# Expert pairs of a hybrid block: the combination moved behind the gathers, other accumulator banks first, and gate and up in four runs

## The chip, the cores and the metric

One core of a Trainium2 chip runs the whole program. The metric is device time in microseconds (us) of one execution; the time before is the median of three runs. PE is TensorE (PEld its weight loads), DVE is VectorE, ACT is ScalarE, POOL is GpSimd, SP is SyncE, which issues the weight loads.

## What is computed

A transformer block on 512 tokens of width 1024 in float32: an mLSTM branch and a forgetting-attention branch that are merged, a cross attention, and a mixture of 32 experts of which each token uses two, with a last normalisation. The change lies in the experts:

```python
for e in range(N_EXPERTS):                                  # 32
    he = jax.nn.silu(t @ w_gate[e]) * (t @ w_up[e])         # 1024 -> 512
    y = y + combine[:, e:e + 1] * (he @ w_down[e])          # 512 -> 1024
```

`t` is the normalised input, and `combine` holds each token's weight for each expert, zero for all but two.

## The kernel before

The parts ahead of the experts (branches, attention, router) end at about 790 us of the span and are not touched. The experts run as 16 pairs (`NPAIR`), loop at L1108. An expert takes at most 64 tokens (`CAP`) in a pass, so the two experts of a pair lie side by side in the 128 columns or partitions of one tile. A further loop for experts with more tokens follows the pairs and is not entered in the profiled execution.

For each pair PE does five kinds of work:

- **Gather** (`stationary`, L1012): the tokens of the next pair are picked out of the normalised input `xn` by a matmul with a matrix of zeros and ones, `G` (made by POOL, L1030). A call handles four of the eight blocks of 128 input channels with 32 matmuls (L1019) into one `pss` bank; DVE then scales it to `st` (L1021). Two calls a pair.
- **Gate and up** (`gate_up`, L1037): 16 steps. A step multiplies one block of channels of both experts' tokens with a row block of each expert's matrix; the two matmuls of a step use 64 columns of the array each and run side by side (L1044, `64x512` in the order, `128*64` in the profile, where each matmul has two records). Steps 0 to 7 take gate for the first expert and up for the second, steps 8 to 15 the other two. The results stay in two `acc` banks until all 16 are done.
- **SiLU, product and transposes** (`act`, L1047, and `turned`, L1054): ACT makes `gl` (L1050), DVE `ul` (L1051), PE transposes `ul` into a `pss` bank (L1057), ACT copies it to `hT` (L1059). The transposes are done in the next pair.
- **Down** (`down`, L1062): 16 matmuls with the 64-wide form (L1068) into two `pso` banks; ACT and DVE weight the results and split them into `yh` (L1078) and `yl` (L1079).
- **Combination** (`combine`, L1087): the rows go back to their tokens by matmuls with a matrix of zeros and ones, `C` (POOL, L1084). For each of four blocks of 128 tokens and each half of the width there is a new bank with two matmuls (L1094 with `yh`, L1095 with `yl`), and DVE adds it to the block in SBUF (L1096). One call to `advance(cb, 4)` does four banks, that is two blocks of tokens.

Work of three pairs is interleaved: in pair p PE does gate and up of p, transposes, down and combination of p - 1, and the gathers for p + 1. The generators `gu`, `down` and `cb` are advanced by hand, and the order of PE is the order of the code (it is under a manual schedule); a scheduler orders DVE, ACT, POOL and SP. The order of PE in a pair is: four steps of gate and up, transposes, four steps, down, four steps, first gather, two steps, four banks of combination, two steps, second gather, four banks of combination.

PSUM has four banks for `acc`, two for `pss` and two for `pso`; each call takes the next bank of its kind in turn and waits until its last reader is done. `pss` serves the transposes, the gathers and the combination, `pso` down and the combination. `combine` takes the kind by `banks[tb % len(banks)]`, so with its default `(pss, pso)` the even blocks of tokens go to `pss`.

The 201 MB of expert weights stream through a ring of buffers in SBUF in loads of 1 MiB (or two of 512 KiB), in a fixed order (`Experts.order`): a load is issued by SP (L930, L935) when the matmuls that read its buffer before are done.

Of the kernel before, what the change touches and what calls it, by code (L numbers as in the profile page):

```python
# [953 lines left out]
def run_experts(ex, pe, both, ctx, tc, a, X2, dram, small, acc, pss, pso, left, right, ident, rpow, wp, c, mraw):  # L954
    nc = tc.nc
    V, S, G, TE, SP = nc.vector, nc.scalar, nc.gpsimd, nc.tensor, nc.sync
    iot, iot64, Eb, Ab, rk, tokf, wsl = c.iot, c.iot64, c.Eb, c.Ab, c.rk, c.tokf, c.wsl
# [7 lines left out]
    def weight_parts():  # L965

        wpt = c.wparts
        dn = sg.tile([P, NB], F32, name="dn")
        V.scalar_tensor_tensor(dn, c.dv, 1.0, c.gs, op0=OP.add, op1=OP.mult)
        V.reciprocal(wf[:, :, 0], dn)  # L970
        V.tensor_mul(wf[:, :, 1], wf[:, :, 0], c.dv)
        rem = sg.tile([P, NB, 2], F32, name="rem")
        V.tensor_copy(wpt[:, :, :, 0], wf)
        V.tensor_sub(rem, wf, wpt[:, :, :, 0])
        V.tensor_copy(wpt[:, :, :, 1], rem)
        V.tensor_sub(rem, rem, wpt[:, :, :, 1])
        V.tensor_copy(wpt[:, :, :, 2], rem)
        V.tensor_mul(Vw, Eb.rearrange("p b j e -> p (b j) e")[:, :, None, :].to_broadcast([P, 2 * NB, 3, NE]),
                     wpt.rearrange("p b j a -> p (b j) a")[:, :, :, None].to_broadcast([P, 2 * NB, 3, NE]))

    def weights():

        pw = pss()
        for i in range(2 * NB):
            TE.matmul(pw[:, :3 * NE], c.R[:, i // 2, i % 2], Vw[:, i].rearrange("p a e -> p (a e)"),
                      start=i == 0, stop=i == 2 * NB - 1)
        pwv = pw[:, :3 * NE].rearrange("p (v a b) -> p v a b", v=3, b=2)
        for h in range(2):
            r = slice(h * 64, h * 64 + 64)
            V.tensor_copy(wsl[r], pwv[r, 2, :, h])  # L990
            V.tensor_add(wsl[r], wsl[r], pwv[r, 1, :, h])
            V.tensor_add(wsl[r], wsl[r], pwv[r, 0, :, h])

    def counts():

        pc = pss()
        for tb in range(NB):
            TE.matmul(pc[:, :NE], onesb, Ab[:, tb], start=tb == 0, stop=tb == NB - 1)
        cnt = sg.tile([P, NE], F32, name="cnt")
        V.tensor_copy(cnt, pc[:, :NE])  # L1000
        nt = sg.tile([P, NE], F32, name="nt")
        V.tensor_scalar(nt, cnt, CAP + 0.5, None, op0=OP.is_gt)
        for k in range(2, T // CAP):
            V.scalar_tensor_tensor(nt, cnt, k * CAP + 0.5, nt, op0=OP.is_gt, op1=OP.add)
        inc = sg.tile([P, NE], F32, name="inc")
        V.memset(cnt, 0.0)
        V.tensor_tensor_scan(inc, nt, cnt, 0.0, OP.add, OP.add)
        nov = sg.tile([P, 1], I32, name="nov")
        V.tensor_copy(nov, inc[:, NE - 1:NE])
        return nt, inc, nov  # L1010

    def stationary(G_, g, n=P, pt=None):  # L1012

        st = sg.tile([P, 4, n], F32, name="st", tag="st", bufs=4)
        if pt is None:
            pt = pss()
            for j in range(4):
                for i in range(2 * NB):
                    TE.matmul(pt[:, j * n:(j + 1) * n], c.XN[:, i % 2, i // 2, (4 * g + j) * P:(4 * g + j + 1) * P],  # L1019
                              G_[:, i // 2, :n], start=i == 0, stop=i == 2 * NB - 1)  # L1020
        V.tensor_mul(st, pt[:, :4 * n].rearrange("p (j t) -> p j t", j=4),  # L1021
                     c.gsc[:, 4 * g:4 * g + 4, None].to_broadcast([P, 4, n]))
        return st

    def slots_of(p):
        G_ = sg.tile([P, NB, P], F16, name="G", tag="G", bufs=2)
        for tb in range(NB):
            for i in range(2):
                e = 2 * p + i
                G.tensor_scalar(G_[:, tb, i * 64:i * 64 + 64], iot[:, :64], c.code[:, tb, e:e + 1], None,  # L1030
                                op0=OP.is_equal)
        return G_
# [4 lines left out]
    def gate_up(sts, ws, ps):  # L1037


        for ph in range(2):  # L1040
            for k in range(KB):
                for h, w in enumerate(ws):
                    i = (ph + h) % 2
                    TE.matmul(ps[i][half(h)], sts[k // 4][:, k % 4, half(h)], w[i][k], start=k == 0, stop=k == KB - 1)  # L1044
                yield
# [8 lines left out]
    def turned(ul, r):  # L1054
        pt = pss()
        for j in range(4):
            TE.transpose(pt[:, j * r:(j + 1) * r], ul[:r, j::4], ident[:r, :r])  # L1057
        hT = sg.tile([P, 4, r], F32, name="hT", tag="hT", bufs=1)
        S.activation(hT, pt[:, :4 * r].rearrange("p (j t) -> p j t", j=4), AF.Copy)  # L1059
        return hT  # L1060

    def down(hT, ws, o):  # L1062

        for j in range(4):
            for x in range(2):
                for h, w in enumerate(ws):
                    n = (x + h) % 2
                    TE.matmul(o[n][half(h)], hT[:, j, half(h)], w[j][:, n * 512:(n + 1) * 512],  # L1068
                              start=j == 0, stop=j == 3)
                yield  # L1070

    def weigh(o, wcol, k=P):

        yh = wp.tile([P, D], F32R, name="yh", tag="wraw", bufs=3)
        yl = wp.tile([P, D], F32R, name="yl", tag="wraw", bufs=3)
        for n in range(2):
            c = slice(n * 512, (n + 1) * 512)
            S.activation(yh[:k, c], o[n][:k], AF.Copy, scale=wcol)  # L1078
            V.scalar_tensor_tensor(yl[:k, c], o[n][:k], wcol, yh[:k, c].bitcast(F32), op0=OP.mult, op1=OP.subtract)  # L1079
        return yh, yl  # L1080

    def places(tokcol, k=P):
        C = sg.tile([P, T], F32R, name="C", tag="C", bufs=2)
        G.tensor_scalar(C[:k], iot[:k], tokcol, None, op0=OP.is_equal)  # L1084
        return C

    def combine(yh, yl, C, k=P, banks=(pss, pso)):  # L1087

        for tb in range(NB):
            ts = slice(tb * P, (tb + 1) * P)  # L1090
            for n in range(2):
                c = slice(n * 512, (n + 1) * 512)
                o = banks[tb % len(banks)]()
                TE.matmul(o, C[:k, ts], yh[:k, c], start=True, stop=False)  # L1094
                TE.matmul(o, C[:k, ts], yl[:k, c], start=False, stop=True)  # L1095
                V.tensor_add(X2[tb][:, c], X2[tb][:, c], o)  # L1096
                yield

    def advance(g, n=99):
        for _ in range(n):  # L1100
            if g is None or next(g, "end") == "end":
                return

    ex.load(len(ex.order))
    with pe:
        sts = [stationary(c.G0, g, pt=c.pts[g]) for g in range(2)]
        before = None
        for p in range(NPAIR):  # L1108
            es = (2 * p, 2 * p + 1)
            ps = [acc(), acc()]  # L1110
            gu = gate_up(sts, [(ex.rows(e, 0), ex.rows(e, 1)) for e in es], ps)
            if p == 0:
                advance(gu, 6)
                for f in (c.codes, c.numbers):
                    for h in range(2):
                        f(h)
                weight_parts()
                both.close()
            if p + 1 < NPAIR:
                G_ = slots_of(p + 1)  # L1120
            C = places(tokf[:, p:p + 1])
            advance(gu, 4 if p else 2)
            cb = None
            if before:
                hT = turned(before[0], P)
            advance(gu, 4 if p else 0)
            if before:
                o = [pso(), pso()]
                advance(down(hT, [ex.rows(e, 2) for e in before[1]], o))
                cb = combine(*weigh(o, wsl[:, p - 1:p]), before[2])  # L1130
            advance(gu, 4)
            if p == 0:
                weights()
            if p == 1:
                nt, inc, nov = counts()
            nst = []
            if p + 1 < NPAIR:
                nst.append(stationary(G_, 0))
            advance(gu, 2)
            advance(cb, 4)  # L1140
            advance(gu, 2)
            if p + 1 < NPAIR:
                nst.append(stationary(G_, 1))
            advance(cb, 4)
            before = act(ps, P), es, C
            sts = nst
        hT = turned(before[0], P)
        o = [pso(), pso()]
        advance(down(hT, [ex.rows(e, 2) for e in before[1]], o))
        C = before[2]  # L1150
# [5 lines left out]
    with tc.If(n_ov > 0):  # L1156
        with left("ov") as ov:
# [52 lines left out]
            with tc.For_i(0, n_ov, 1) as it:  # L1210
# [12 lines left out]
                o = [acc(), acc()]  # L1223
# [4 lines left out]
    cb = combine(*weigh(o_last, wsl[:, NPAIR - 1:NPAIR]), C, banks=(acc,))  # L1228
# [55 lines left out]
```

## Time and profile before

| | |
|---|---|
| median of three runs | 1293.26 us (1292.9 to 1294.54) |
| profiled execution, its own time | 1293.15 us |
| its span | 1291.3 us |
| PE busy | 1247.0 us, 97% |
| DVE busy | 552.9 us, 43% |
| ACT busy | 355.8 us, 28% |
| POOL busy | 130.5 us, 10% |
| chain that ended last | PE 93%, DVE 3%, ACT 1% |
| read from HBM | 275.08 MB |

The span runs from the first to the last instruction on the core; the execution's own time has a little around it. Rows of the timeline give the start, the length, the engine, the line, the operation, its tiles and shapes, how many were merged, and in square brackets the idle time of the engine ahead of it with what ended it. Ends of matmuls are modelled, so the distance between the starts of two matmuls says more than their lengths.

### The profile page before, as it was taken

What the parts mean: (1) busy time and instruction counts of PE and PEld (TensorE: products, weight loads), DVE (VectorE), ACT (ScalarE), POOL (GpSimd) and SP (SyncE); (2) the same over time, 40 slices, a digit from 0 to 9 for tenths busy, and PEclk for the clock granted to TensorE, in tenths of its full rate; (3) what the DMA queues carried; (4) which work ended last, traced back from release to release, by engine and by line L of the source; (5) the groups of instructions that cost most, each with busy time, mean ns of one, the idle gap of its engine ahead of it and who ended that gap; (6) DMA issues with size and microseconds to landing.
All of it is one profiled execution on the core that took longest, in us unless ns stands there. A gap on an engine that the chain in (4) does not pass through costs nothing.

```text
span 1291.3 us, 18633 instructions
## 1 busy us (share of the span) xinstructions
PE 1247.0 (97%) x7606; PEld 896.2 (69%) x7606; DVE 552.9 (43%) x1045; ACT 355.8 (28%) x627; POOL 130.5 (10%) x250
## 2 busy tenths in 40 slices
PE   6999999999999999999999997999999999999995
PEld 5898999888888987899977994444444444444443
DVE  4437455334566654356645537232332222222325
ACT  4435344222344433234433443000000000000002
POOL 0001011000001010001000003111122111111001
PEclk9999999999999999999999998999999999999998
DMA  4352432344245325333531266999999999999971
GB/s 168 85 112 83 79 93 75 95 86 103 82 86 79 93 68 171 95 124 111 173 98 49 92 284 236 407 417 418 417 417 418 418 418 416 416 416 419 417 324 66
DMA packets 99113, 278.45 MB, mean 216 GB/s; under 512 B 6196, under 2 KB 67908, under 8 KB 77904
## 3 DMA queue, kind: packets, MB, share of 16 engines
q1 hardware_dynamic: 97536, 272.46, 58.6%
q0 software_dynamic: 1488, 4.76, 1.1%
q8 instruction: 61, 1.00, 0.3%
q14 instruction: 28, 0.23, 0.1%
HBM read 275.08 MB, written 2.12 MB: 215 GB/s over the span
## 4 chain that ended last, share of the span: by engine, by line
PE 93%; DVE 3%; ACT 1%; issue 1%; DMA 1%; SPq 0%; POOL 0%; POOLq 0%; DVEq 0%; ACTq 0%
PE acc L1044 18%; PE acc L103 16%; PE acc L105 16%; PE acc L104 16%; PE pso L1068 9%; PE pss L1019 4%; PE pss L1094 1%; PE pso L1095 1%; PE pso L1094 1%; PE pss L103 1%; PE pss L105 1%; PE pss L104 1%; PE pss L1057 1%; PE pss L1095 1%; DVE st L1021 1%
## 5 line engine op out<-in xcount | busy, mean ns | idle before, releaser
L1044 PE MATMUL acc<-mw,st 128*64 128x512 f32 x880 | 236.7, 600 | 0.4 <-DVE st L1021 0.4
L125 DVE TENSOR_TENSOR wl<-wraw,wh 128x1024 fp32r<-128x1024 f32 x120 | 146.9, 1225 | 184.7 <-ACT wh L124 180.0
L124 ACT ACTIVATE wh<-wraw 128x1024 fp32r<-128x1024 f32 x120 | 126.8, 1058 | 193.9 <-PE acc L104 93.3
L1044 PEld LDWEIGHTS acc<-mw,st 128*64 128x64 f32 x880 | 67.3, 137 | 108.7 <-issue 103.8
L103 PE MATMUL acc<-hH,wh 128*128 128x512 f32 x320 | 128.5, 401 | 0.0
L104 PE MATMUL acc<-hL,wh 128*128 128x512 f32 x320 | 127.8, 399 | 0.0
L105 PE MATMUL acc<-hH,wl 128*128 128x512 f32 x320 | 125.8, 400 | 1.7 <-DVE wl L125 1.7
L1079 DVE SCALAR_TENSOR_TENSOR yl<-pso,wsl,yh 128x512 fp32r<-128x512 f32 x32 | 22.6, 746 | 225.4 <-ACT yh L1078 225.4
L1068 PE MATMUL pso<-mw,hT 128*64 128x512 f32 x440 | 112.6, 592 | 0.7 <-ACT hT L1059 0.7
L104 PE MATMUL acc<-wl,hH 128*128 128x256 f32 x384 | 109.4, 285 | 0.9 <-DVE wl L125 0.9
L103 PE MATMUL acc<-wh,hH 128*128 128x256 f32 x384 | 109.3, 286 | 0.9 <-ACT wh L124 0.9
L105 PE MATMUL acc<-wh,hL 128*128 128x256 f32 x384 | 109.2, 285 | 0.2 <-DVE hL L196 0.2
L1030 POOL TENSOR_SCALAR G<-iot,code 128x64 f16<-128x64 f32 x120 | 51.0, 452 | 322.8 <-PE pss L1019 311.1
L1068 PEld LDWEIGHTS pso<-mw,hT 128*64 128x64 f32 x440 | 37.1, 137 | 61.4 <-issue 59.2
L104 PEld LDWEIGHTS acc<-wl,hH 128*128 128x128 f32 x384 | 73.1, 190 | 1.8 <-DVE wl L125 1.4
L103 PEld LDWEIGHTS acc<-wh,hH 128*128 128x128 f32 x384 | 72.9, 190 | 1.7 <-ACT wh L124 1.3
L105 PEld LDWEIGHTS acc<-wh,hL 128*128 128x128 f32 x384 | 73.2, 191 | 0.5 <-DVE hL L196 0.4
L105 PEld LDWEIGHTS acc<-hH,wl 128*128 128x128 f32 x320 | 60.7, 190 | 15.9 <-DVE wl L125 2.2
L104 PEld LDWEIGHTS acc<-hL,wh 128*128 128x128 f32 x320 | 60.7, 190 | 13.3
L103 PEld LDWEIGHTS acc<-hH,wh 128*128 128x128 f32 x320 | 60.6, 189 | 13.4 <-ACT wh L124 0.4
L1019 PEld LDWEIGHTS <-xn 128*128 128x128 f16 x960 | 53.7, 98 | 22.7 <-issue 22.7
L1078 ACT ACTIVATE yh<-pso,wsl 128x512 fp32r<-128x512 f32 x32 | 20.3, 684 | 154.4 <-PE pso L1068 154.4
(320 smaller groups left out, 2333.5 us busy)
## 6 DMA issues: line engine op xcount, KB each, us to landing
mw<-w_gate SPq DMA_DIRECT2D x55, 1024.0 KB, 14.7
mw<-w_up SPq DMA_DIRECT2D x55, 1024.0 KB, 13.4
mw<-w_down SPq DMA_DIRECT2D x55, 1024.0 KB, 11.7
wraw<-w_in SPq DMA_DIRECT2D x64, 512.0 KB, 5.5
wraw<-w_xkv SPq DMA_DIRECT2D x16, 512.0 KB, 3.4
mwh<-w_up SPq DMA_DIRECT2D x10, 512.0 KB, 11.1
mwl<-w_gate SPq DMA_DIRECT2D x10, 512.0 KB, 10.1
mwh<-w_down SPq DMA_DIRECT2D x10, 512.0 KB, 12.0
```

The costliest lines, as they stand in the source:

```text
L103: TE.matmul(out, ah, bh, start=start, stop=False, **kw)
L104: TE.matmul(out, ah, bl, start=False, stop=False, **kw)
L105: TE.matmul(out, al, bh, start=False, stop=stop, **kw)
L124: S.activation(h, raw, AF.Copy)
L125: V.tensor_sub(l, raw, h.bitcast(F32))
L1019: TE.matmul(pt[:, j * n:(j + 1) * n], c.XN[:, i % 2, i // 2, (4 * g + j) * P:(4 * g + j + 1) * P], G_[:, i // 2, :n], start=i == 0, stop=i ...
L1030: G.tensor_scalar(G_[:, tb, i * 64:i * 64 + 64], iot[:, :64], c.code[:, tb, e:e + 1], None, op0=OP.is_equal)
L1044: TE.matmul(ps[i][half(h)], sts[k // 4][:, k % 4, half(h)], w[i][k], start=k == 0, stop=k == KB - 1)
L1068: TE.matmul(o[n][half(h)], hT[:, j, half(h)], w[j][:, n * 512:(n + 1) * 512], start=j == 0, stop=j == 3)
L1079: V.scalar_tensor_tensor(yl[:k, c], o[n][:k], wcol, yh[:k, c].bitcast(F32), op0=OP.mult, op1=OP.subtract)
L1094: TE.matmul(o, C[:k, ts], yh[:k, c], start=True, stop=False)
L1095: TE.matmul(o, C[:k, ts], yl[:k, c], start=False, stop=True)
```

## The change

`combine` gets `banks=(pso, pss)`: the even blocks of tokens go to `pso`, the odd ones to `pss`. The first half of the combination moves ahead of two steps of gate and up, so that it follows on the first gather as the second half does on the second gather, and the last four steps of gate and up form one run. The same instructions are issued.

```diff
             if before:
                 o = [pso(), pso()]
                 advance(down(hT, [ex.rows(e, 2) for e in before[1]], o))
-                cb = combine(*weigh(o, wsl[:, p - 1:p]), before[2])
+                cb = combine(*weigh(o, wsl[:, p - 1:p]), before[2], banks=(pso, pss))
             advance(gu, 4)
...
             if p + 1 < NPAIR:
                 nst.append(stationary(G_, 0))
-            advance(gu, 2)
             advance(cb, 4)
-            advance(gu, 2)
+            advance(gu, 4)
             if p + 1 < NPAIR:
                 nst.append(stationary(G_, 1))
             advance(cb, 4)
```

PE in pair 2, from the second step of the two that follow the first gather (before). `pss_8446` is the bank of that gather; the numbers count tiles, not banks.

```order
L1044 MATMUL acc_8357<-mw_7762,st_8318 64x512
L1094 MATMUL pss_8484<-yh_8411,C_8246 128x512
L1095 MATMUL pss_8484<-yl_8412,C_8246 128x512
L1094 MATMUL pss_8488<-yh_8411,C_8246 128x512
L1095 MATMUL pss_8488<-yl_8412,C_8246 128x512
L1094 MATMUL pso_8492<-yh_8411,C_8246 128x512
L1095 MATMUL pso_8492<-yl_8412,C_8246 128x512
L1094 MATMUL pso_8496<-yh_8411,C_8246 128x512
L1095 MATMUL pso_8496<-yl_8412,C_8246 128x512
L1044 MATMUL acc_8358<-mw_7760,st_8318 64x512
```

The same place in the changed kernel, from the last matmul of the first gather:

```order
L1019 MATMUL pss_8446<-G_8359,xn16_7195 128x128
L1094 MATMUL pso_8480<-yh_8411,C_8246 128x512
L1095 MATMUL pso_8480<-yl_8412,C_8246 128x512
L1094 MATMUL pso_8484<-yh_8411,C_8246 128x512
L1095 MATMUL pso_8484<-yl_8412,C_8246 128x512
L1094 MATMUL pss_8488<-yh_8411,C_8246 128x512
L1095 MATMUL pss_8488<-yl_8412,C_8246 128x512
L1094 MATMUL pss_8492<-yh_8411,C_8246 128x512
L1095 MATMUL pss_8492<-yl_8412,C_8246 128x512
L1044 MATMUL acc_8358<-mw_7760,st_8318 64x512
L1044 MATMUL acc_8357<-mw_7762,st_8318 64x512
```

The four matmuls (two steps) that stood between the gather and the combination now stand behind it, at the head of a run of eight.

PE in the same pair at the second half of the combination, before; `pss_8505` is the bank of the second gather:

```order
L1019 MATMUL pss_8505<-G_8359,xn16_7195 128x128
L1094 MATMUL pss_8539<-yh_8411,C_8246 128x512
L1095 MATMUL pss_8539<-yl_8412,C_8246 128x512
L1094 MATMUL pss_8543<-yh_8411,C_8246 128x512
L1095 MATMUL pss_8543<-yl_8412,C_8246 128x512
L1094 MATMUL pso_8547<-yh_8411,C_8246 128x512
L1095 MATMUL pso_8547<-yl_8412,C_8246 128x512
L1094 MATMUL pso_8551<-yh_8411,C_8246 128x512
L1095 MATMUL pso_8551<-yl_8412,C_8246 128x512
L1044 MATMUL acc_8559<-mw_7764,st_8445 64x512
```

In the changed kernel:

```order
L1019 MATMUL pss_8505<-G_8359,xn16_7195 128x128
L1094 MATMUL pso_8539<-yh_8411,C_8246 128x512
L1095 MATMUL pso_8539<-yl_8412,C_8246 128x512
L1094 MATMUL pso_8543<-yh_8411,C_8246 128x512
L1095 MATMUL pso_8543<-yl_8412,C_8246 128x512
L1094 MATMUL pss_8547<-yh_8411,C_8246 128x512
L1095 MATMUL pss_8547<-yl_8412,C_8246 128x512
L1094 MATMUL pss_8551<-yh_8411,C_8246 128x512
L1095 MATMUL pss_8551<-yl_8412,C_8246 128x512
L1044 MATMUL acc_8559<-mw_7764,st_8445 64x512
```

With two `pss` banks in turn, the second `pss` tile behind a gather takes the gather's own bank: before `pss_8543`, the second of the four tiles, now `pss_8551`, the fourth.

DVE in a later pair (the tiles are named as above, `x1_4532` is the block of tokens that is added to), before:

```order
L1021 TENSOR_TENSOR st_9719<-pss_9720,gsc_5640 128x512
L1096 TENSOR_TENSOR x1_4532<-x1_4532,pss_9758 128x512
L1096 TENSOR_TENSOR x1_4532<-x1_4532,pss_9762 128x512
L1096 TENSOR_TENSOR x1_4532<-x1_4532,pso_9766 128x512
L1096 TENSOR_TENSOR x1_4532<-x1_4532,pso_9770 128x512
L1051 TENSOR_TENSOR ul_9830<-acc_9652,gl_9829 128x512
L1021 TENSOR_TENSOR st_9778<-pss_9779,gsc_5640 128x512
L1096 TENSOR_TENSOR x1_4532<-x1_4532,pss_9813 128x512
```

In the changed kernel:

```order
L1021 TENSOR_TENSOR st_9719<-pss_9720,gsc_5640 128x512
L1096 TENSOR_TENSOR x1_4532<-x1_4532,pso_9754 128x512
L1096 TENSOR_TENSOR x1_4532<-x1_4532,pso_9758 128x512
L1096 TENSOR_TENSOR x1_4532<-x1_4532,pss_9762 128x512
L1096 TENSOR_TENSOR x1_4532<-x1_4532,pss_9766 128x512
L1051 TENSOR_TENSOR ul_9830<-acc_9652,gl_9829 128x512
L1021 TENSOR_TENSOR st_9778<-pss_9779,gsc_5640 128x512
L1096 TENSOR_TENSOR x1_4532<-x1_4532,pso_9813 128x512
```

The places on DVE are the same, `st` ahead of the four additions in both; only the banks that the additions read are exchanged.

## The prediction

> **What bounds the kernel now.** I read the page first, then the stretches, then what TensorE waits for, then one expert pair in order of time, last the weight loads. The page's head and its two DMA rows:
>
> ```profile
> span 1291.3 us, 18633 instructions
> PE 1247.0 (97%) x7606; PEld 896.2 (69%) x7606; DVE 552.9 (43%) x1045; ACT 355.8 (28%) x627; POOL 130.5 (10%) x250
> DMA  4352432344245325333531266999999999999971
> GB/s 168 85 112 83 79 93 75 95 86 103 82 86 79 93 68 171 95 124 111 173 98 49 92 284 236 407 417 418 417 417 418 418 418 416 416 416 419 417 324 66
> ```
>
> The first 24 slices are PE with little DMA; from slice 25 on, where the experts run, both look full. The same in three stretches of 50 us (columns: length, busy time and count of PE, PEld, DVE, ACT, POOL, granted clock, DMA share, GB/s):
>
> ```profile
> 850.00:900.00 50.00, 49.74 (x296) 21.55 (x293) 10.71 (x17) 4.33 (x7) 4.87 (x9) 1.00 1.01 417
> 1000.00:1050.00 50.00, 49.74 (x297) 21.05 (x293) 10.54 (x16) 4.32 (x7) 5.40 (x10) 1.00 1.02 418
> 1200.00:1250.00 50.00, 49.48 (x292) 22.34 (x290) 14.78 (x23) 3.65 (x6) 3.13 (x2) 1.00 1.01 417
> ```
>
> PE is at full clock and busy for 99%, and DMA is at 417 GB/s: two candidates for the bound. The SiLU (L1050) runs once a pair and so gives the period; the second row below is all that PE waited for in the pairs:
>
> ```profile
> L1050 ACT ACTIVATE gl<-acc x13: 597/597/597, 873.0 to 1235.2; 128x512 f32<-128x512 f32 x13
> PE pss L1094 <- DVE st L1021: 3.6, 14, 0.3
> ```
>
> (1235.2 - 873.0) / 12 = 30.18 us a pair. PE never waits for a weight; its one wait, in 14 pairs, is for `st` (the scaling of the gather) before a combination matmul. So PE sets the pace, and what counts is the distance from one PE start to the next. One pair in order of time (start, length, line, idle before):
>
> ```profile
> 1016.04 1.96 PE L1019 MATMUL pss<-G,xn 128*128 128x128 f16 x32
> 1017.93 1.94 PE L1044 MATMUL acc<-mw,st 128*64 128x512 f32 x8
> 1019.79 0.50 PE L1094 MATMUL pss<-yh,C 128*128 128x512 f32 x1
> 1020.13 0.40 PE L1095 MATMUL pss<-yl,C 128*128 128x512 f32 x1
> ...
> 1021.54 0.39 PE L1095 MATMUL pso<-yl,C 128*128 128x512 f32 x1
> 1021.86 1.94 PE L1044 MATMUL acc<-mw,st 128*64 128x512 f32 x8
> 1023.73 1.96 PE L1019 MATMUL pss<-G,xn 128*128 128x128 f16 x32
> 1025.50 0.48 PE L1094 MATMUL pss<-yh,C 128*128 128x512 f32 x1
> 1025.82 0.40 PE L1095 MATMUL pss<-yl,C 128*128 128x512 f32 x1
> 1026.47 0.50 PE L1094 MATMUL pss<-yh,C 128*128 128x512 f32 x1 [0.26 <-DVE st L1021]
> 1026.81 0.40 PE L1095 MATMUL pss<-yl,C 128*128 128x512 f32 x1
> ...
> 1027.74 0.40 PE L1095 MATMUL pso<-yl,C 128*128 128x512 f32 x1
> 1028.08 0.64 PE L1044 MATMUL acc<-mw,st 128*64 128x512 f32 x1
> ...
> 1031.66 0.75 PE L1057 MATMUL pss<-ident,ul 128*128 128x128 f32 x4
> ```
>
> From start to start: first gather 1.89, two steps of gate and up 1.86, first combination 2.07, two steps 1.87, second gather 1.77, second combination 2.58, and four steps in one run (1028.08 to 1031.66) 3.58. Both combinations are eight matmuls. In the first they follow each other by (1021.54 - 1020.13) / 6 = 0.235 us. In the second the third matmul comes 0.65 after the second and the fourth 0.34 after that: it writes the `pss` bank that the gather just filled and that `st` still reads. The idle column shows 0.26 us of this, because matmul ends are modelled; start to start the price is (0.65 - 0.235) + (0.34 - 0.235) = 0.52.
>
> **The change part by part.** From the first gather to the end of the second combination the pair takes 1.89 + 1.86 + 2.07 + 1.87 + 1.77 + 2.58 = 12.04 us. After it there are a gather, a combination, four steps, a gather, a combination.
>
> - Gather straight into a combination: before, the second gather did this, 1.77. The first one, which went into gate and up, took 1.89. Saves 0.12.
> - Four steps in one run instead of two and two: 3.58 (the row 1028.08, which also follows a combination and goes into full-width matmuls) for 1.86 + 1.87 = 3.73. Saves 0.15: one change from full-width matmuls to the 64-wide ones and back is gone.
> - Banks `pso`, `pso`, `pss`, `pss`: without the wait a combination takes 0.32 to its second matmul (1025.50 to 1025.82), 6 x 0.235 and 0.32 from its last to gate and up (1021.54 to 1021.86), 2.05 in all; the first combination's 2.07 bounds it from above. The second saves 2.58 - 2.05 = 0.53, the first 0.02.
>
> Sum: 1.77 + 2.05 + 3.58 + 1.77 + 2.05 = 11.22, 0.82 us less a pair. Pair 0 has no combination and its two runs were one already; the last pair has no gathers, so it keeps its number of runs. That leaves 14 pairs, as many as the waits row counts: 14 x 0.82 = 11.5 us. With 2.07 for each combination it would be 0.78 and 10.9. The other bound: the first combination now begins in a bank that no other engine still has, and if its 0.32 to the second matmul became 0.235, that would save 0.085 more, 14 x 0.085 = 1.2 us; both rows show 0.32 to 0.34, so I don't count it.
>
> Does the wait come back elsewhere? DVE's rows in the same pair:
>
> ```profile
> 1013.42 1.41 DVE L1079 SCALAR_TENSOR_TENSOR yl<-pso,wsl,yh 128x512 fp32r<-128x512 f32 x2 [14.48 <-ACT yh L1078]
> 1018.03 0.69 DVE L1021 TENSOR_TENSOR st<-pss,gsc 128x512 f32<-128x512 f32 x1 [3.20 <-PE pss L1019]
> 1020.57 1.29 DVE L1096 TENSOR_TENSOR x<-x,pss 128x512 f32<-128x512 f32 x2 [1.84 <-PE pss L1095]
> 1025.72 0.69 DVE L1021 TENSOR_TENSOR st<-pss,gsc 128x512 f32<-128x512 f32 x1 [0.54 <-PE pss L1019]
> ```
>
> `st` starts 0.22 us after a combination that follows its gather, and PE got the bank at +0.97 (1026.47 - 1025.50). In the new order that bank is the fourth, due with the seventh matmul at 0.32 + 5 x 0.235 = +1.50: 0.53 to spare. The third bank was read long before. The first two are `pso`: for the first combination `yl` has read them by 1014.83, 3 us before it can start (1016.04 + 1.77); for the second, the first one's additions have. The additions (two in 1.29, so 0.60 each behind each other) stand behind `st` on DVE: they end by about 0.91 + 4 x 0.60 + 0.08 = +3.4, and the next gather wants a `pss` bank at 2.05 + 3.58 = +5.6. SiLU and `ul` come after the same four steps and before the same gather as now. Nothing is added to POOL, ACT or SP; SP only sees buffers freed earlier.
>
> What is late next is the weights: DMA is at 417 GB/s already, and a pair's twelve loads of 1 MiB (12.58 MB) take 12.58 / 0.417 = 30.2 us, as long as PE takes now and longer than the 29.4 it will. The faster PE therefore eats the lead of the loads, 0.8 us a pair. The last pair shows how large it is (issues on SP, their times to landing in two stretches of two issues each, and the users on PE):
>
> ```profile
> 1224.42 0.38 SPq L930 DMA_DIRECT2D mw<-w_gate  x1
> DMA to landing us min/median/max: 13.7/14.7/15.8
> 1227.85 0.38 SPq L930 DMA_DIRECT2D mw<-w_gate  x1
> DMA to landing us min/median/max: 15.3/16.3/17.3
> 1253.99 5.32 PE L1044 MATMUL acc<-mw,st 128*64 128x512 f32 x24
> 1259.24 0.50 PE L1094 MATMUL pss<-yh,C 128*128 128x512 f32 x1
> ```
>
> The load of 1224.42 lands by 1240.2 and is first used by the run at 1253.99: 13.8 us of lead, 2.3 after the change. The one of 1227.85 lands by 1245.2, is used from the fifth of the six steps of that run (1253.99 + 4 x 0.875 = 1257.5), lead 12.3; in the new order the first combination, 2.05, goes ahead of it, which leaves 12.3 + 2.05 - 11.5 = 2.9. So the whole gain fits, barely: it is hidden by the lead, and costs come back at once where the loads slip by more than 2.3 us.
>
> The Trainium skill, HBM Reference, Specifications (TRN2), has a rule against hoping for more: a core that streams alone gets about 425 GB/s, bounded by its DMA engines. The trace's 417 agrees. An estimate by that page: 12.58 MB / 425 GB/s = 29.6 us a pair, still more than 29.4, so loads would not catch up either.
>
> **The rivals.**
>
> *Some weights come late.* For it: 2.3 us is less than one load's spread (13.7 to 15.8 within two). Against it: leads only shrink towards the end, so a slip costs once. A slip of 3 to 5 us costs 1 to 3: 1282.5 to 1284.7.
>
> *The loads pace every pair.* For it: the flat 417 GB/s and 30.2 us for a pair's loads. A saved microsecond of PE would turn into waiting, and the time would stay, 1293.2. This is what the skill's figure means if there is no lead. Against it: PE has no wait for a load, and 13.8 us of lead.
>
> *Slower: the wait for `st` stays and both combinations have it.* Each directly follows a gather now, as only the second did. If both then cost 2.58, the pair takes 1.77 + 2.58 + 3.58 + 1.77 + 2.58 = 12.28, 0.24 more: 14 x 0.24 = 3.4 us, 1296.7. It decides at `st` ending 0.53 us later than now, which it would if DVE took an addition (0.60) first; against it, `st` stands ahead of the additions and its input is ready sooner.
>
> *Only half works.* If the stall merely moves to another bank in the second combination, the two run savings are left: 0.12 + 0.15 + 0.02 = 0.29, 4.1 us, 1289.2.
>
> **How the numbers follow.** The profiled execution took 1293.15 us (span 1291.3 and 1.85 around it), the median is 1293.26, 0.1 above. Forecast 1293.26 - 11.5 = 1281.8. Chances: forecast 0.85, late weights 0.07, loads pace every pair 0.02, only half 0.03, slower 0.03. A measurement of this kernel tells about 0.2%, 2.6 us, from no change. Faster: 0.85 + 0.07 + 0.03 = 0.95; same 0.02; slower 0.03. The range: from the bound above, 1281.8 - 1.2 = 1280.6, up to the late weights, 1284.7; with 0.85 + 0.07 in it, it leaves out the three other cases, 0.08.
>
> **What would show it.** Right: the period of L1050 at 29.37 us, no wait for `st` on L1094, 2.05 to 2.07 for each combination, 3.58 for each run of four steps, and PE's end chain unchanged behind the last pair. Leads of 2 to 3 us in the last pair. Wrong: waits of PE for DMA on L1044 or L1068, first in the last pairs (weights); a gap before the seventh matmul of a combination (`st`); a gap before its first (`pso`).

## The result and the profile after

The changed kernel takes 1283.01 us (median of four runs, 1282.39 to 1283.14) against 1293.08 for the kernel before (four runs, 1292.65 to 1294.54): ratio 0.9922, interval 0.9911 to 0.9934, so 10.1 us less. Forecast were 1281.8 and 11.5 less. The profiled execution took 1283.09 with a span of 1281.4.

The stretches first (length, busy time and count of PE, PEld, DVE, ACT, POOL, granted clock, DMA share, GB/s):

```profile
850.00:900.00 50.00, 50.00 (x300) 22.55 (x300) 12.74 (x20) 4.33 (x7) 4.85 (x9) 1.00 1.01 417
1000.00:1050.00 50.00, 50.00 (x320) 23.04 (x317) 13.43 (x21) 4.33 (x7) 4.85 (x9) 1.00 1.02 417
1200.00:1250.00 50.00, 50.00 (x276) 21.23 (x274) 12.49 (x20) 4.32 (x7) 2.46 (x2) 1.00 1.01 416
```

In these stretches PE has no idle time left, the clock is still 1.00, and DMA moves what it moved before, 417 GB/s. The SiLU's row over twelve periods, and PE's waits from 800 to 1262 us that last at least 0.5:

```profile
L1050 ACT ACTIVATE gl<-acc x13: 597/597/597, 872.4 to 1224.8; 128x512 f32<-128x512 f32 x13
PE pss L1057 <- DVE x L1096: 1.2, 1, 1.2
PE pso L1068 <- ACT hT L1059: 0.7, 1, 0.7
```

(1224.8 - 872.4) / 12 = 29.37 us a pair, the forecast to the hundredth. The wait of L1094 for `st` is gone. A new one is there, once: the transposes (L1057) wait 1.2 us for an addition. The last row, down behind the last transposes, is no cost of the change: the kernel before has it too, 0.75 us at 1266.77. The same pair as before in order of time:

```profile
1013.43 0.48 PE L1094 MATMUL pso<-yh,C 128*128 128x512 f32 x1
...
1014.92 0.39 PE L1094 MATMUL pss<-yh,C 128*128 128x512 f32 x1
...
1015.48 3.65 PE L1044 MATMUL acc<-mw,st 128*64 128x512 f32 x16
1019.06 1.96 PE L1019 MATMUL pss<-G,xn 128*128 128x128 f16 x32
1020.83 0.48 PE L1094 MATMUL pso<-yh,C 128*128 128x512 f32 x1
...
1022.55 0.40 PE L1095 MATMUL pss<-yl,C 128*128 128x512 f32 x1
1022.88 0.64 PE L1044 MATMUL acc<-mw,st 128*64 128x512 f32 x1
...
1026.46 0.75 PE L1057 MATMUL pss<-ident,ul 128*128 128x128 f32 x4
```

Both combinations take 2.05 (1013.43 to 1015.48, 1020.83 to 1022.88), the run of four steps 3.58, the gather 1.77. The seventh matmul, which takes the gather's bank, starts at 1014.92, +1.49. On DVE `st` ends ahead of it:

```profile
1013.66 0.69 DVE L1021 TENSOR_TENSOR st<-pss,gsc 128x512 f32<-128x512 f32 x1 [3.20 <-PE pss L1019]
1014.27 1.27 DVE L1096 TENSOR_TENSOR x<-x,pso 128x512 f32<-128x512 f32 x2
```

1013.66 + 0.69 = 1014.35, 0.57 us before the seventh matmul, without an idle mark on PE. The new wait stands in the last pair. After, on PE and on DVE:

```profile
1252.26 0.50 PE L1094 MATMUL pso<-yh,C 128*128 128x512 f32 x1
...
1254.01 0.39 PE L1095 MATMUL pss<-yl,C 128*128 128x512 f32 x1
1255.57 0.75 PE L1057 MATMUL pss<-ident,ul 128*128 128x128 f32 x4 [1.18 <-DVE x L1096]
```

```profile
1253.64 0.68 DVE L1051 TENSOR_TENSOR ul<-acc,gl 128x512 f32<-128x512 f32 x1
1254.24 0.68 DVE L1096 TENSOR_TENSOR x<-x,pso 128x512 f32<-128x512 f32 x1
1254.84 1.27 DVE L1096 TENSOR_TENSOR x<-x,pss 128x512 f32<-128x512 f32 x2
```

Before, the same place on PE and on DVE:

```profile
1264.91 0.40 PE L1095 MATMUL pso<-yl,C 128*128 128x512 f32 x1
1265.28 0.74 PE L1057 MATMUL pss<-ident,ul 128*128 128x128 f32 x4
```

```profile
1264.54 0.68 DVE L1051 TENSOR_TENSOR ul<-acc,gl 128x512 f32<-128x512 f32 x1
1265.14 0.68 DVE L1096 TENSOR_TENSOR x<-x,pss 128x512 f32<-128x512 f32 x1
```

From the last combination matmul to the transposes it was 0.37 us (they waited for `ul`, which ended at 1265.22) and is 1.56 now, although `ul` ends at 1254.32: the transposes need a `pss` bank, and both `pss` banks are read by the last two additions in DVE's queue. The first is read until about 1254.84 + 0.68 = 1255.52. In all other pairs a run of four steps lies between. So the transposes come 1.56 - 0.37 = 1.2 us later than with the old banks.

The lead of the weights, in the row of the load that was the tightest in the forecast, its time to landing, and its first use:

```profile
1220.89 0.33 SPq L930 DMA_DIRECT2D mw<-w_gate  x1
DMA to landing us min/median/max: 18.8/18.8/18.8
1243.09 3.60 PE L1044 MATMUL acc<-mw,st 128*64 128x512 f32 x16
```

It lands at 1239.7 (before: 1240.2), 3.4 us ahead of that run. This distance from a load's landing to its first use is its lead.

### The profile page after: what moved, and what is told of

The parts are those of the page before. It is cut to its first block, busy times and chain, and to the rows that moved or that the text cites. A ratio compares the mean times of both kernels' runs of the same rounds, so it can differ in the third digit from the quotient of the medians.

```text
span 1281.4 us, 18617 instructions
## 1 busy us (share of the span) xinstructions
PE 1239.1 (97%) x7606; PEld 897.1 (70%) x7606; DVE 549.2 (43%) x1045; ACT 355.9 (28%) x627; POOL 130.6 (10%) x250
## 4 chain that ended last, share of the span: by engine, by line
PE 94%; DVE 3%; ACT 1%; issue 1%; DMA 1%; POOL 0%; SPq 0%; POOLq 0%; DVEq 0%; ACTq 0%
PE acc L1044 18%; PE acc L103 17%; PE acc L105 17%; PE acc L104 17%; PE pso L1068 9%; PE pss L1019 4%; PE pso L1094 1%; PE pso L1095 1%; PE pss L1095 1%; PE pss L1094 1%; PE pss L103 1%; PE pss L105 1%; PE pss L104 1%; PE pss L1057 1%; PE pso L103 1%
## 5 line engine op out<-in xcount | busy, mean ns | idle before, releaser
L1044 PE MATMUL acc<-mw,st 128*64 128x512 f32 x880 | 232.7, 597 | 0.6 <-DVE st L1021 0.6
```

## The experiments

**The banks alone.** The kernel before with

```diff
-                cb = combine(*weigh(o, wsl[:, p - 1:p]), before[2])
+                cb = combine(*weigh(o, wsl[:, p - 1:p]), before[2], banks=(pso, pss))
```

> The banks alone (pso, then pss), with the order of before: gather, two steps, combination, two steps, gather, combination. Theory (the gain is a sum of independent parts: the wait for st 0.53 us a pair, the moved steps 0.29 a pair, less 1.2 once in the last pair, where the transposes follow the combination directly and now need a pss bank that the additions still hold): 14 x 0.53 - 1.2 = 6.2 us less than before, 1286.9, period 29.66 us, no wait for st. Rival (the two parts only work together, because the first combination can't hide its banks unless it follows the gather): no more than 4 us. Rival (the 1.2 us missing from the forecast is not the last pair's but chance): 7.4 us less, 1285.7.

Measured: 1286.69 us (1286.18 to 1287.53), before 1293.37 (13 runs): ratio 0.9948, interval 0.9931 to 0.9964, 6.7 us less. Period, and PE's longest wait in the pairs:

```profile
L1050 ACT ACTIVATE gl<-acc x13: 597/597/598, 872.5 to 1228.6; 128x512 f32<-128x512 f32 x13
PE pss L1057 <- DVE x L1096: 1.2, 1, 1.2
```

(1228.6 - 872.5) / 12 = 29.68 us, 0.51 less than before's 30.18 in the rows. The banks act without the move, and they alone bring the wait of the last pair. The total alone would not tell the theory's 6.2 us from the second rival's 7.4; the row of the wait does.

**The move alone.** The changed kernel with the banks of before:

```diff
-                cb = combine(*weigh(o, wsl[:, p - 1:p]), before[2], banks=(pso, pss))
+                cb = combine(*weigh(o, wsl[:, p - 1:p]), before[2])
```

> The order alone (the first combination follows its gather, gate and up in four runs), with the banks of before (pss, then pso). Theory: both combinations now wait for st, each 2.58 us instead of 2.07 and 2.58, while the moved steps save 0.27: 0.24 us a pair more, 14 x 0.24 = 3.4 us slower, 1296.5; the transposes of the last pair start 0.38 us after its last combination matmul as before. Rival (the first gather's st is ready in time, since DVE has less queued there than at the second): 0.27 a pair less, 3.8 us faster, 1289.3.

Measured: 1296.21 us (1294.94 to 1297.30, ten runs), ratio 1.0021, interval 1.0011 to 1.0030, 2.8 us slower. The wait of the combination for `st`, and the first combination of a pair:

```profile
PE pss L1094 <- DVE st L1021: 7.3, 28, 0.3
```

```profile
989.00 0.48 PE L1094 MATMUL pss<-yh,C 128*128 128x512 f32 x1
989.32 0.39 PE L1095 MATMUL pss<-yl,C 128*128 128x512 f32 x1
989.97 0.50 PE L1094 MATMUL pss<-yh,C 128*128 128x512 f32 x1 [0.26 <-DVE st L1021]
...
991.57 0.64 PE L1044 MATMUL acc<-mw,st 128*64 128x512 f32 x1
```

28 waits instead of 14, and the first combination takes 991.57 - 989.00 = 2.57 like the second. This is the forecast's slower rival, with its mechanism and about its price (3.4 forecast; the profiled execution, counted from the first pair's SiLU as further below, has 3.5): the same move costs time with one order of banks and saves it with the other.

**The last pair.** The changed kernel with

```diff
-banks=(pso, pss))
+banks=(pso, pss) if p + 1 < NPAIR else (pss, pso))
```

> The changed kernel, with the banks of before in the last pair alone (it has no gather, so nothing there waits for st). Theory: the transposes start 0.38 us after the last combination matmul again instead of 1.57, and the whole is 1.2 us faster than the changed kernel: 1281.8 (11.3 to 11.5 us less than before). Rival (the end of the last pair is hidden by something else that ends as late, such as the down matrices' last loads or ul): 1283.0, as the changed kernel.

Measured: 1281.58 us (1280.72 to 1282.88), ratio 0.9911, interval 0.9895 to 0.9928. Its last combination matmul and the transposes:

```profile
1252.49 0.40 PE L1095 MATMUL pso<-yl,C 128*128 128x512 f32 x1
1252.87 0.75 PE L1057 MATMUL pss<-ident,ul 128*128 128x128 f32 x4
```

0.38 us again. The two medians differ as expected, but their intervals overlap; so both were run once more on one chip.

> The changed kernel once more, on the same chip and beside the same runs of the kernel before as the two below. Both theories: 1283.0 as at first, 0.8% less than before, period 29.37 us, one wait of 1.2 us of the transposes in the last pair.

> The version with the old banks in the last pair, once more, to set it beside the changed kernel on one chip. Theory (the wait of the transposes for a pss bank is all that separates them): 1.2 us less than the changed kernel, 1281.8. Rival (the wait only moves): the same as the changed kernel.

Measured beside the same runs of before (1292.75): 1282.81 for the changed kernel (0.9919, interval 0.9905 to 0.9933), 1281.19 for the other (0.9913, interval 0.9899 to 0.9927). Twice the medians differ by 1.4 to 1.6 in the expected direction; the intervals still overlap, and what carries the verdict is the row of the wait, there in both profiled executions of the changed kernel and in neither of the other.

Most of the scatter stands ahead of the pairs: in the nine profiled executions of this document the first pair's SiLU starts between 813.94 and 816.14 us. From there to the end of the span both executions of the changed kernel take 465.9 us, and both with the last pair mended 465.0. So 0.9 of the 1.2 us reach the end, and the rival has the rest: with the old banks half of the next down matmuls start 0.3 us behind the others (1267.07 and 1266.77 in the kernel before), just when the last addition frees their `pso` bank (1265.74 + 1.28 = 1267.02).

**How much the loads still allow.** The changed kernel with half of each gather:

```diff
-                for i in range(2 * NB):
+                for i in range(0, 2 * NB, 2):
```

> The changed kernel with half of the gather: the matmuls that gather the low parts of the split input are left out (16 instead of 32 in a call), so the tokens are picked with the high part alone. TensorE has 16 x 0.056 = 0.9 us less a gather, 30 gathers, 27 us in all. Theory (the loads run at their full rate, and the changed kernel has 3.85 us of lead left at the tightest load of the last pair): only the lead can be gained, PE waits for loads, 1283.0 - 3.9 = 1279.1, and the period goes to 30.2 us once the lead is gone. Rival (loads speed up or were not at their limit): 1256 with a period of 27.6.

Measured: 1279.07 us (1277.46 to 1283.81), ratio 0.9897, interval 0.9873 to 0.9921. PE's waits, then some SiLUs, one a pair:

```profile
PE acc L1044 <- DMA mw<-w_gate: 9.4, 7, 1.4
PE pso L1068 <- DMA mw<-w_down: 2.7, 4, 1.2
```

```profile
868.32 0.60 ACT L1050 ACTIVATE gl<-acc 128x512 f32<-128x512 f32 x1 [8.71 <-PE acc L1044]
895.92 0.60 ACT L1050 ACTIVATE gl<-acc 128x512 f32<-128x512 f32 x1 [8.73 <-PE acc L1044]
...
1006.84 0.60 ACT L1050 ACTIVATE gl<-acc 128x512 f32<-128x512 f32 x1 [9.32 <-PE acc L1044]
...
1248.35 0.60 ACT L1050 ACTIVATE gl<-acc 128x512 f32<-128x512 f32 x1 [9.98 <-PE acc L1044]
```

The period is 27.60 at first. The last eight, once the lead is used up, are between 28.74 and 31.39 and (1248.35 - 1006.84) / 8 = 30.19 in the mean, as the theory has it. TensorE has 27 us less to do, and about 4 of it reach the end: 3.9 between the medians, with an interval of some 3 us to either side, and 4.5 between the profiled executions from the first gather of the pairs (809.85 and 810.28) to the end. So the loads bound this version, and it gained the lead of 3.4 and the 1.2 us by which the load of that lead landed earlier here (at 1219.44 + 19.5, counted from the first gather, against 1220.89 + 18.8). Why it did is open. The expectation's lead of 3.85 adds 0.45 to the 3.4 of the rows, for which they show no ground: the two matmuls of a step start together.

**A further step.** The version with the last pair mended, and the transposes moved from between two runs of gate and up to between the second gather and the second combination of the pair before:

```diff
-            if before:
-                hT = turned(before[0], P)
             advance(gu, 4 if p else 0)
...
                 nst.append(stationary(G_, 1))
+                ul = act(ps, P)
+                hT = turned(ul, P)
             advance(cb, 4)
-            before = act(ps, P), es, C
+            if p + 1 == NPAIR:
+                ul = act(ps, P)
+            before = ul, es, C
```

> The version with the old banks in the last pair, and in all pairs but the last the four transposes stand between the second gather and the second combination instead of between two runs of gate and up, so that two runs of four steps become one of eight. A transposing group costs 0.52 + 0.46 + 0.21 - 0.42 = 0.78 us between two runs; between a gather and a combination, where no 64-wide matmul stands beside it, about 0.5. Theory (each change to the 64-wide matmuls and back costs about 0.27, and loads bind only when 3.85 us of lead are used up): 15 x 0.27 = 4.0 us less than the version it starts from, 1277.7, which takes nearly all the lead; a few waits for loads of under 1 us in all in the last pairs. Rival (ul is late for the transposes: SiLU, then DVE, 1.45 us behind the end of gate and up, against 1.77 for the gather): a wait on L1057 in every pair, 1281 or more. Rival (loads bind earlier): 1279 with waits of several us for loads.

Measured: 1278.84 us (1278.38 to 1279.88), ratio 0.9891, interval 0.9875 to 0.9906, the fastest of all with the whole computation in it. SiLUs at the start and the end:

```profile
871.62 0.60 ACT L1050 ACTIVATE gl<-acc 128x512 f32<-128x512 f32 x1 [9.61 <-PE acc L1044]
900.63 0.60 ACT L1050 ACTIVATE gl<-acc 128x512 f32<-128x512 f32 x1 [9.61 <-PE acc L1044]
...
1191.88 0.60 ACT L1050 ACTIVATE gl<-acc 128x512 f32<-128x512 f32 x1 [10.76 <-PE acc L1044]
1221.89 0.60 ACT L1050 ACTIVATE gl<-acc 128x512 f32<-128x512 f32 x1 [10.60 <-PE acc L1044]
```

The period falls to 29.01, 0.36 a pair where 0.27 were expected, and is 30.01 at the end. `ul` was not late: PE has no wait on L1057 in the pairs. What holds it up in the last three pairs stands under PEld, which waits for `w_gate`:

```profile
PEld acc L1044 <- DMA mw<-w_gate: 2.6, 3, 1.0
```

15 x 0.36 = 5.4 us are more than the lead, which in the version it started from is 3.2 (issued at 1221.66, landed 18.6 later, used at 1243.42). So the loads bind in the last pairs, and the gain over that version is 2.4 to 2.7 between the medians instead of 4.0, and 2.2 from the first pair's SiLU to the end. That is the second rival's time, and both have a part in it: the larger saving meets the loads, and the load of that lead also lands 0.9 later, counted from the first pair's SiLU (1222.11 + 18.6 from 815.38, against 1221.66 + 18.6 from 815.78), which leaves 2.3 us of the lead. Why it lands later is open.

## Why the prediction was nearly right

- **What bounds the kernel** held. PE's starts set the pace, not the full DMA: 0.82 us less on PE a pair is 0.82 less in the period.
- **The sum a pair** held to 0.01 us, and its parts are shown apart: the banks 0.53 forecast and 0.51 measured alone; the move worth 0.29 with the new banks (29.68 - 29.37 = 0.31 measured) and a loss with the old ones. Counted from the first pair's SiLU to the end of the span, the banks alone save 6.3 us (6.2 expected).
- **Where the wait would go:** the margin of `st` was forecast as 0.53 and is 0.57 to the seventh matmul. The banks of `pso` were free, the next gather found its bank.
- **The lead of the weights** was forecast as 2.3 us and is 3.4. Half of the difference is the load, which landed 0.5 earlier; why is not known. The other half is PE, which came 0.6 later than 1253.99 - 11.5 = 1242.5, and 0.5 of that is from ahead of the expert pairs, where the two profiled executions differ in code that is the same: the first pair's SiLU starts at 814.94 us before and at 815.46 after.

```profile
814.94 0.60 ACT L1050 ACTIVATE gl<-acc 128x512 f32<-128x512 f32 x1 [22.32 <-PE acc L1044]
```

```profile
815.46 0.60 ACT L1050 ACTIVATE gl<-acc 128x512 f32<-128x512 f32 x1 [21.46 <-PE acc L1044]
```

- **The step that failed** is "PE's end chain unchanged behind the last pair". The prediction followed `pss` to the next gather, with four steps of gate and up between, and took it that the last pair costs nothing because it has no gather. But there the transposes follow on the combination directly, and they take a `pss` bank. With `pso` first, both `pss` banks are read last: the transposes wait 1.2 us, and the end comes 0.9 later.
- **Luck.** The time lies in the range, but 1.2 us above the forecast, in the part that was kept for late weights. No weight was late; the wait of the last pair and 0.5 us from ahead of the pairs fell where that room was.
- **Smaller slips.** DMA is full from slice 26 on, not 25: slices 24 and 25 move 284 and 236 GB/s. The spread quoted for late weights, 13.7 to 15.8, is 2.1 us and so less than the lead of 2.3, not more. A slip of 5 us would cost 5 - 2.3 = 2.7, so the range would end at 1284.5 instead of 1284.7.

The spans agree with this account: 14 x 0.82 = 11.5, less 0.9, less the 0.5 ahead of the pairs, is 10.1, and they differ by 1291.3 - 1281.4 = 9.9.

The Trainium skill's figure in the HBM Reference, Specifications (TRN2), about 425 GB/s for a core that streams alone, stands beside a bound that the runs now show. Without lead a pair takes 30.2 us here, 12.58 MB / 30.19 us = 417 GB/s, 2% below that figure. By the Trainium skill's figure, with its estimate of 29.6 us a pair, the prediction's rival of loads that pace every pair would have come out faster than before, and not at the same time.

## What to carry to other kernels

When a matmul must wait for a bank that another engine still reads, give it first the banks that nobody holds, and follow each bank to its next user in every iteration, the last one too, where the usual neighbour is missing. Price such a wait from start to start; the idle column showed half of it. When DMA is full and PE still sets the pace, look up the lead of the loads at their first use: about that is what a faster PE can gain (here 2.2 and 4.5 us, with leads of 3.2 and 3.4, since the loads themselves came about 1 us later or earlier).

## What the runs showed of the hardware

The same four transposes cost different amounts by their place. Between two runs of the 64-wide matmuls, in the changed kernel (matmuls of such a run start 0.43 apart):

```profile
1231.53 0.59 PE L1044 MATMUL acc<-mw,st 128*64 128x512 f32 x1
...
1232.06 0.75 PE L1057 MATMUL pss<-ident,ul 128*128 128x128 f32 x4
...
1232.74 0.64 PE L1044 MATMUL acc<-mw,st 128*64 128x512 f32 x1
...
1233.22 0.59 PE L1044 MATMUL acc<-mw,st 128*64 128x512 f32 x1
```

From the first row to the last it is 1.69 us where two starts in a row would take 0.86, so the transposes cost 0.83 there. The expectation had 0.78, without the slower start of the run behind them (0.48 from 1232.74 to 1233.22 instead of 0.43). Between a gather and a combination, both full-width, the last version has:

```profile
987.52 1.96 PE L1019 MATMUL pss<-G,xn 128*128 128x128 f16 x32
989.32 0.70 PE L1057 MATMUL pss<-ident,ul 128*128 128x128 f32 x4
989.77 0.47 PE L1094 MATMUL pso<-yh,C 128*128 128x512 f32 x1
```

From the gather's start to the combination's it is 2.25, against 1.77 without them: 0.48, and about 0.5 was expected. The difference, 0.83 - 0.48 = 0.35, is the saving of 0.36 a pair.
